# A hybrid mLSTM/RG-LRU block with 32 experts: part of the conditioning scale summed on VectorE, with another order in the first regions

## The chip, the cores and the metric

The kernel runs on one core of one Trainium2 chip. The metric is the time of one execution on the device in microseconds; a kernel's figure is the median of its runs. The profile is that of one execution, and its times count from the first instruction.

## What is computed

One layer of a streaming encoder, on 256 frames of 2048 features, in float32. The part that matters here is the beginning:

```python
mod = jax.nn.silu(c) @ w_ada[l] + b_ada[l]
sh1, sc1, g1, sh2, sc2, g2 = jnp.split(mod, 6, axis=-1)
hn = rmsnorm(x) * (1.0 + sc1[:, None]) + sh1[:, None]
mix = hybrid_mixer(hn, w_in[l], ...)          # proj = hn @ w_in, then mLSTM heads and RG-LRU blocks, then w_out
x = x + g1[:, None] * mix
hn = rmsnorm(x) * (1.0 + sc2[:, None]) + sh2[:, None]
x = x + g2[:, None] * hier_moe(hn, ...)       # 32 experts, the two best of one group for each frame
y = rmsnorm(x) * final_g
```

c is one vector of 2048, w_ada is 2048 x 12288: six conditioning vectors of 2048 features. The scale sc1 (section 1) and the shift sh1 (section 0) are needed before the first product with w_in (2048 x 6152) can be made.

## The kernel before

All weights come through one queue (SyncE) in chunks of 1 MB into a ring of seven buffers; SyncE and TensorE work in the order in which the code is written, VectorE and ScalarE in an order that a scheduler sets when the program is built. It is fixed then: each engine takes its instructions one after the other.

The features of the model dimension are worked in four groups of 512, the regions (kk = 0 to 3). For a group the kernel needs that part of the scale and of the shift, both 512 values. Each is a product of silu(c) with 2048 x 512 of w_ada, 4 chunks. ada_now (L253) makes it on TensorE: per chunk four products in which 32 columns hold one column of cz (silu(c)) and the 512 columns of w_ada pass by, so four partial sums of the row end up on partitions 0, 32, 64 and 96 of one PSUM tile. ada_quarters (L261) then adds the bias row (L264, VectorE) and turns the row into four columns of 128 with four products with one column (L269), which also add the four partial sums; L271 (VectorE) writes them to ada. A product in f32 shows as two instructions in the profile.

x_transposed (L361) transposes the normalised x of the group by TensorE (L366), and ScalarE multiplies by the scale while it copies to xT (L368). modulate (L373) adds the shift: ScalarE writes the rounded sum HH (L375), VectorE what is left, HL (L376). by_channel (L469) is one chunk of w_in: split (L463) makes its rounded half on ScalarE (L465) and its low half on VectorE (L466), each for two of the chunk's four slices at a time, into one of three buffers ws; then 48 products follow, in threes: HH with the rounded half (L481), HL with the rounded half (L482), HH with the low half (L483).

Region 0's scale and shift come first and nothing overlaps them. Then, in region kk = 0, 1 and 2, the kernel makes three chunks of w_in products (go(0), go(1), go(2), for three groups of output columns whose sums stay in PSUM) and in between, by hand-written order, the scale and shift of region kk + 1: eight chunks of w_ada. So a region asks for eleven chunks. The order is go(0), three chunks of the scale, go(1), the fourth, two chunks of the shift, the scale's columns, the transposes, two chunks of the shift, its row, go(2) with the shift's columns and modulate in its middle. In the third of these regions (kk = 2, EARLY) go(2) stands ahead of the last two shift chunks. Region 3 has only its three chunks of w_in. Below, "first", "second" and "third region" are kk = 0, 1 and 2.

Behind that stage come the rest of the products with w_in, the recurrences, the four other sections of the conditioning (ada_later, on VectorE and TensorE, in the buffer acc), w_out, the router, and then the experts in ten rounds, with 32-column products (L1114, L1167) that take their weights straight from the ring.

Of the kernel before, what the change touches and what calls it, by code (L numbers as in the profile page):

```python
# [14 lines left out]
OP = mybir.AluOpType  # L15
# [94 lines left out]
def block_kernel(ctx, tc, x, c, w_ada, b_ada, w_in, b_gates, vec_a, vec_b, w_lru_a, w_lru_x, w_out,  # L110
# [11 lines left out]
    def pb(shape=(128, 512), name="pb"):  # L122
        return psum.tile(list(shape), F32, name=name, tag="b", bufs=2)
# [4 lines left out]
    def st(shape, name, tag=None, bufs=1, dt=F32):  # L128
        return sb.tile(list(shape), dt, name=name, tag=tag or name, bufs=bufs)
# [68 lines left out]
    cs = st([128, NCONST], "cs")  # L198
# [62 lines left out]
    def ada_quarters(sec, n, ps):  # L261
# [8 lines left out]
        one = 1.0 if sec == 1 else 0.0  # L270
        V.tensor_scalar(ada[:, sec, n * 4:n * 4 + 4], pc, one, None, op0=OP.add)  # L271

    def ada_row(sec, k):
        return chunk(w_ada[:, sec * D:sec * D + D].rearrange("(p k) (j n) -> p k j n", k=16, j=4)[:, k])

    acc = st([128, 4, 512], "acc")


    unsummed = []
# [396 lines left out]
    for kk in range(4):  # L676
        go = lambda i, mid=None: by_channel(pss[i], kk, first[i][0], mid)
        if kk == 3:
            for i in range(3):
                go(i)  # L680
            decay()
            SP.dma_start(wlru[:, 0], w_lru_a.rearrange("n c d -> c n d"))
            SP.dma_start(wlru[:, 1], w_lru_x.rearrange("n c d -> c n d"))
            SP.dma_start(cs[:, C_LT:], const[:, C_LT:])
            SP.dma_start(wg, w_in[:, 4096:4104].rearrange("(k p) n -> p k n", p=128))
            SP.dma_start(wr, w_rt.rearrange("(k p) n -> p k n", p=128))
            break
        pss1 = [pb() for _ in range(2)]
        a1, a0 = (ada_now(sec, kk + 1, p) for sec, p in zip((1, 0), pss1))
        q1, q0 = (ada_quarters(sec, kk + 1, p) for sec, p in zip((1, 0), pss1))  # L690
        go(0)
        for _ in range(3):
            next(a1)
        go(1)
        next(a1)
        next(q1)
        next(a1, None)
        next(a0)
        next(a0)
        next(q1, None)  # L700
        x_transposed(4 * kk + 4)
        early = kk in EARLY
        if early:
            go(2)
        next(a0)
        next(a0)
        next(q0)

        def mid():
            next(q0, None)  # L710
            modulate(kk + 1)

        if early:
            mid()
        else:
            go(2, mid)
# [626 lines left out]
```

## Time and profile before

| | us |
|---|---|
| median of 3 runs | 1347.98 (1347.59 to 1357.47) |
| the profiled execution | 1349.25 |
| its span, first to last instruction | 1347.4 |
| TensorE busy | 1161.2 |
| VectorE busy | 545.1 |
| ScalarE busy | 350.5 |

The profiled execution's time is 1.85 us longer than its span. In the profile PE is TensorE, PEld its weight loads, DVE VectorE, ACT ScalarE, SP SyncE. An instruction's row gives its start and its duration; in square brackets stands the time that its engine was idle before it, and what ended that. Matmuls overlap each other, so their pace is read from one start to the next and not from the duration.

### The profile page before, as it was taken

How to read it: one execution, taken by the hardware profiler on the slowest of the kernel's cores; microseconds unless marked ns; L12 is line 12 of the kernel's file. 1: busy time of each engine (PE TensorE's matmuls, PEld its weight loads, DVE VectorE, ACT ScalarE, POOL GpSimd, SP SyncE). 2: the span in 40 equal slices, each digit the busy share in tenths (PEclk: the TensorE clock that was granted, in tenths of full speed). 3: DMA queues.
4: the chain of work that ended last, by engine and by line, in shares of the span. 5: the costliest groups of instructions: out<-in, count | busy, mean ns of one | idle time of the engine just before them, and what ended most of it. 6: DMA issues, size and time to landing. Idle time of an engine off the chain costs nothing. (4 is left out here: it accounts for less than half of the span.)

```text
span 1347.4 us, 19862 instructions
## 1 busy us (share of the span) xinstructions
PE 1161.2 (86%) x8002; PEld 668.1 (50%) x8002; DVE 545.1 (40%) x985; ACT 350.5 (26%) x557; POOL 5.6 (0%) x13
## 2 busy tenths in 40 slices
PE   4898999999999999999777898878885688887886
PEld 0667889987877888543132434223341133422332
DVE  1333667779869877523013131302140013130214
ACT  2232494545446443521010111001010010100103
POOL 0000000000000000000000000000000000000000
PEclk9999999999989999899899999999997889998998
DMA  9999869689969998989999999999997999999995
GB/s 335 375 375 365 270 221 338 239 328 344 365 246 405 408 375 322 359 353 403 423 423 423 422 423 423 423 424 423 424 423 312 424 424 422 423 423 424 423 413 217
DMA packets 116896, 504.81 MB, mean 375 GB/s; under 512 B 12425, under 2 KB 14761, under 8 KB 69185
## 3 DMA queue, kind: packets, MB, share of 16 engines
q1 hardware_dynamic: 114832, 496.97, 92.4%
q0 software_dynamic: 720, 5.24, 0.9%
q8 instruction: 64, 1.05, 0.3%
q10 hardware_dynamic: 1248, 1.29, 0.3%
q14 instruction: 32, 0.25, 0.0%
HBM read 526.54 MB, written 2.10 MB: 392 GB/s over the span
## 5 line engine op out<-in xcount | busy, mean ns | idle before, releaser
L1114 PE MATMUL pa<-ring,XE 128*32 128x512 f32 x1368 | 224.6, 631 | 59.0 <-DMA ring<-in_w_e_up_dram 33.3
L466 DVE TENSOR_TENSOR ws<-ring,ws 128x1024 fp32r<-128x1024 f32 x128 | 154.8, 1219 | 65.1 <-ACT ws L465 64.6
L465 ACT ACTIVATE ws<-ring 128x1024 fp32r<-128x1024 f32 x128 | 134.4, 1058 | 164.8 <-PE pa L497 76.2
L481 PE MATMUL pa<-HH,ws 128*128 128x256 f32 x512 | 151.6, 296 | 3.6 <-ACT ws L465 1.9
L483 PE MATMUL pa<-HH,ws 128*128 128x256 f32 x512 | 148.9, 291 | 5.0 <-DVE ws L466 5.0
L1114 PE MATMUL pa<-early,XE 128*32 128x512 f32 x656 | 135.0, 624 | 20.9 <-DMA early<-in_w_e_up_dram 12.6
L1114 PEld LDWEIGHTS pa<-ring,XE 128*32 128x32 f32 x1368 | 60.1, 115 | 183.4 <-issue 93.2
L482 PE MATMUL pa<-HL,ws 128*128 128x256 f32 x512 | 148.7, 290 | 1.4 <-DVE HL L376 1.4
L1114 PE MATMUL pa<-more,XE 128*32 128x512 f32 x536 | 109.4, 614 | 14.5 <-DMA more<-in_w_e_up_dram 14.5
L977 ACT ACTIVATE XE<-pb,adx 128x128 f32<-128x128 f32 x80 | 36.6, 457 | 304.4 <-DVE XE L980 304.4
L1167 PE MATMUL pa<-ring,hT 128*32 128x512 f32 x640 | 106.0, 598 | 11.1 <-DMA ring<-in_w_e_down_dram 11.0
L1146 DVE TENSOR_TENSOR hs<-hs,pa 128x512 f32<-128x512 f32 x10 | 6.9, 688 | 264.0 <-PE pa L1114 264.0
L481 PEld LDWEIGHTS pa<-HH,ws 128*128 128x128 f32 x512 | 101.8, 199 | 18.5 <-issue 8.4
L483 PEld LDWEIGHTS pa<-HH,ws 128*128 128x128 f32 x512 | 101.7, 199 | 6.6 <-DVE ws L466 6.6
L482 PEld LDWEIGHTS pa<-HL,ws 128*128 128x128 f32 x512 | 101.8, 199 | 2.0 <-DVE HL L376 1.9
L325 DVE SCALAR_TENSOR_TENSOR acc<-ring,cz,acc 128x1024 f32<-128x1024 f32 x78 | 98.1, 1276 | 0.9 <-DMA ring<-in_w_ada_dram 0.8
L1134 DVE TENSOR_TENSOR X<-X,pa 128x512 f32<-128x512 f32 x80 | 51.9, 682 | 91.6 <-PE pa L1132 91.6
L973 PE MATMUL pb<-two,XN 128*128 128x128 f32 x640 | 77.3, 279 | 6.7 <-ACT hT L1153 6.7
L973 PEld LDWEIGHTS pb<-two,XN 128*128 128x128 f32 x640 | 73.1, 192 | 18.9 <-issue 9.2
L1114 PEld LDWEIGHTS pa<-early,XE 128*32 128x32 f32 x656 | 34.0, 113 | 79.5 <-issue 38.1
L1125 ACT ACTIVATE ys<-y 128x512 fp32r<-128x512 f32 x40 | 25.2, 630 | 181.1 <-DVE y L1123 181.1
L1167 PE MATMUL pa<-more,hT 128*32 128x512 f32 x304 | 57.1, 594 | 4.0 <-DMA more<-in_w_e_down_dram 4.0
(378 smaller groups left out, 1379.1 us busy)
## 6 DMA issues: line engine op xcount, KB each, us to landing
ring<-in_w_ada_dram SPq DMA_DIRECT2D x96, 1024.0 KB
ring<-in_w_e_gate_dram SPq DMA_DIRECT2D x62, 1024.0 KB
ring<-in_w_e_down_dram SPq DMA_DIRECT2D x61, 1024.0 KB
ring<-in_w_e_up_dram SPq DMA_DIRECT2D x57, 1024.0 KB
ring<-in_w_in_dram SPq DMA_DIRECT2D x48, 1024.0 KB
early<-in_w_e_up_dram SPq DMA_DIRECT2D x30, 1024.0 KB
more<-in_w_e_down_dram SPq DMA_DIRECT2D x29, 1024.0 KB
more<-in_w_e_up_dram SPq DMA_DIRECT2D x25, 1024.0 KB
```

The lines of the kernel that those rows point to most:

```text
L325: V.scalar_tensor_tensor(o, w[:, h:h + 2], cz[:, k, 3:4], o, op0=OP.mult, op1=OP.add)
L465: A.activation(ws[:, 0], s, AF.Copy)
L466: V.tensor_tensor(ws[:, 1], s, ws[:, 0], op=OP.subtract)
L481: PE.matmul(o, wh[:, cc], HH[:, k], start=k == 0 and ch % 2 == 0, stop=False, skip_group_check=True)
L482: PE.matmul(o, wh[:, cc], HL[:, k], start=False, stop=False, skip_group_check=True)
L483: PE.matmul(o, wl[:, cc], HH[:, k], start=False, stop=k == 15, skip_group_check=True)
L973: PE.matmul(p[:, j], XN[:, h, kk, j], which[:, h], start=h == 0, stop=h == 1)
L977: A.activation(XE[:, k], p[:, j], AF.Identity, scale=adx[:, 1, k:k + 1], bias=adx[:, 0, k:k + 1])
L1114: PE.matmul(o[c0:c0 + width], lhs(kk, j)[:, c0:c0 + width], w[:, j], start=first and j == 0, stop=last and j == 3)
L1125: A.activation(ys[0], y, AF.Copy)
L1134: V.tensor_tensor(X1[:, h, ns], X1[:, h, ns], pc, op=OP.add)
L1167: PE.matmul(pds[n][c0:c0 + width], hT[:, f, c0:c0 + width], w[:, n], start=f == 0, stop=f == 3)
```

## The change

For regions 1 to 3 the scale is no longer a product. ada_vector multiplies each slice of w_ada (128 rows by 512 columns) by its column of cz on VectorE and sums the sixteen slices into acc, which then holds 128 partial sums for each of the 512 features. ada_columns makes columns of them: for each of the four columns one product of the bias row with the column that selects its row, and one of acc with a column of ones, summed in PSUM. The row addition of the scale on VectorE goes. The shift stays as it was.

The order of a region becomes: two chunks of the scale, go(0), two chunks of the scale, one of the shift, go(1), two of the shift, (third region: go(2),) the last of the shift, the scale's columns, the transposes, the shift's row, go(2) with the shift's columns and modulate in its middle.

```diff
+    def ada_vector(sec, n):
+        o = acc[:, n]
+        for kk in range(4):
+            w = ada_w(sec, n, kk)
+            for j in range(4):
+                sc = cz[:, kk * 4 + j, 3:4]
+                if kk + j == 0:
+                    V.tensor_scalar(o, w[:, j], sc, None, op0=OP.mult)
+                else:
+                    V.scalar_tensor_tensor(o, w[:, j], sc, o, op0=OP.mult, op1=OP.add)
+            yield
+
+    def ada_columns(sec, n):
+        pc = pb([128, 4])
+        for j in range(4):
+            js = slice(j * 128, j * 128 + 128)
+            PE.matmul(pc[:, j:j + 1], arow[sec][:, js], cs[:, C_SEL + n:C_SEL + n + 1], start=True, stop=False)
+            PE.matmul(pc[:, j:j + 1], acc[:, n, js], cs[:, C_SEL + 11:C_SEL + 12], start=False, stop=True)
+        one = 1.0 if sec == 1 else 0.0
+        V.tensor_scalar(ada[:, sec, n * 4:n * 4 + 4], pc, one, None, op0=OP.add)
...
-        pss1 = [pb() for _ in range(2)]
-        a1, a0 = (ada_now(sec, kk + 1, p) for sec, p in zip((1, 0), pss1))
-        q1, q0 = (ada_quarters(sec, kk + 1, p) for sec, p in zip((1, 0), pss1))
+        ps0 = pb()
+        a1, a0, q0 = ada_vector(1, kk + 1), ada_now(0, kk + 1, ps0), ada_quarters(0, kk + 1, ps0)
+        for _ in range(2):
+            next(a1)
         go(0)
-        for _ in range(3):
+        for _ in range(2):
             next(a1)
+        next(a0)
         go(1)
-        next(a1)
-        next(q1)
-        next(a1, None)
         next(a0)
         next(a0)
-        next(q1, None)
-        x_transposed(4 * kk + 4)
         early = kk in EARLY
         if early:
             go(2)
         next(a0)
-        next(a0)
+        ada_columns(1, kk + 1)
+        x_transposed(4 * kk + 4)
         next(q0)
```

In the changed kernel the lines lie 21 to 23 further down: the split's halves are L488 and L489 there, the products L504 to L506, HL is L399, the accumulation L283 (first) and L285, the scale's columns L293, L294 and L296.

VectorE at the start of the first region, before; ring_64 is the first chunk of w_in, ws its two halves:

```order
L264 TENSOR_TENSOR row<-pb,brow 128x512
L271 TENSOR_SCALAR ada<-pb 128x4
L466 TENSOR_TENSOR ws<-ring_64,ws 128x1024
L376 SCALAR_TENSOR_TENSOR HL<-xT,ada,HH 128x256 x4
L466 TENSOR_TENSOR ws<-ring_64,ws 128x1024
```

VectorE at the same place in the changed kernel, up to the first w_in chunk, which is ring_66 now; acc is the sum of the scale, ring_64 and ring_65 chunks of w_ada:

```order
L264 TENSOR_TENSOR row<-pb,brow 128x512
L283 TENSOR_SCALAR acc<-ring_64,cz 128x512
L271 TENSOR_SCALAR ada<-pb 128x4
L285 SCALAR_TENSOR_TENSOR acc<-ring_64,cz,acc 128x512
L399 SCALAR_TENSOR_TENSOR HL<-xT,ada,HH 128x256 x4
L285 SCALAR_TENSOR_TENSOR acc<-ring_64,cz,acc 128x512 x2
L285 SCALAR_TENSOR_TENSOR acc<-ring_65,cz,acc 128x512 x4
L489 TENSOR_TENSOR ws<-ring_66,ws 128x1024 x2
```

The low halves of the first w_in chunk stand behind two chunks' accumulations now; one of them stood ahead of HL before.

VectorE from the write of the shift in the middle of the first region's go(2) through the first two w_in chunks of the second region, before:

```order
L271 TENSOR_SCALAR ada<-pb 128x4
L466 TENSOR_TENSOR ws<-ring_68,ws 128x1024
L376 SCALAR_TENSOR_TENSOR HL<-xT,ada,HH 128x256 x4
L466 TENSOR_TENSOR ws<-ring_65,ws 128x1024 x2
L264 TENSOR_TENSOR row<-pb,brow 128x512
L271 TENSOR_SCALAR ada<-pb 128x4
L264 TENSOR_TENSOR row<-pb,brow 128x512
L466 TENSOR_TENSOR ws<-ring_64,ws 128x1024 x2
```

The low half of ring_68 ahead of HL is that of the second region's go(0), ring_65 is its go(1). The same place in the changed kernel, where ring_63 is go(0) and ring_67 go(1):

```order
L271 TENSOR_SCALAR ada<-pb 128x4
L285 SCALAR_TENSOR_TENSOR acc<-ring_68,cz,acc 128x512
L399 SCALAR_TENSOR_TENSOR HL<-xT,ada,HH 128x256 x4
L285 SCALAR_TENSOR_TENSOR acc<-ring_69,cz,acc 128x512 x3
L489 TENSOR_TENSOR ws<-ring_63,ws 128x1024
L285 SCALAR_TENSOR_TENSOR acc<-ring_69,cz,acc 128x512
L489 TENSOR_TENSOR ws<-ring_63,ws 128x1024
L285 SCALAR_TENSOR_TENSOR acc<-ring_64,cz,acc 128x512 x4
L285 SCALAR_TENSOR_TENSOR acc<-ring_65,cz,acc 128x512 x4
L489 TENSOR_TENSOR ws<-ring_67,ws 128x1024 x2
```

Four accumulations and HL stand between the shift's write and go(0)'s first low half, and nine accumulations between that and go(1)'s. The third region has the same pattern.

TensorE behind the first region's go(1), before (L366 are the transposes, L481 the first product of go(2)), and the same place in the changed kernel (L389 are the transposes there, L504 the first product of go(2)):

```order
L258 MATMUL pb<-ring_69,cz 32x512 x4
L258 MATMUL pb<-ring_63,cz 32x512 x4
L258 MATMUL pb<-ring_64,cz 32x512 x4
L269 MATMUL pb<-cs,row 128x1 x4
L366 MATMUL pb<-cs,X 128x128 x8
L258 MATMUL pb<-ring_65,cz 32x512 x4
L258 MATMUL pb<-ring_66,cz 32x512 x4
L481 MATMUL pa<-HH,ws 128x256
```

```order
L258 MATMUL pb<-ring_64,cz 32x512 x4
L258 MATMUL pb<-ring_65,cz 32x512 x4
L258 MATMUL pb<-ring_66,cz 32x512 x4
L293 MATMUL pb<-cs,brow 128x1
L294 MATMUL pb<-cs,acc 128x1
...
L389 MATMUL pb<-cs,X 128x128 x8
L504 MATMUL pa<-HH,ws 128x256
```

Three chunks of the shift instead of five chunks of both lie behind go(1), eight products with one column stand for four, and the transposes are followed by go(2) at once.

## Rows read from the trace of the kernel before

**Rows 1.** The page: busy us (share of the span) and instructions of each engine.
```profile
PE 1161.2 (86%) x8002; PEld 668.1 (50%) x8002; DVE 545.1 (40%) x985; ACT 350.5 (26%) x557; POOL 5.6 (0%) x13
```

**Rows 2.** Busy time by stretches of the span; the columns are in the first line.
```profile
core 0: us, PE busy (x) PEld busy (x) DVE busy (x) ACT busy (x) POOL busy (x), PEclk, DMA share, GB/s
44.00:75.00 31.00, 28.02 (x213) 21.18 (x214) 10.71 (x16) 9.65 (x15) 0.00 (x0) 1.00 1.02 374
106.00:146.00 40.00, 33.90 (x255) 26.79 (x253) 13.40 (x19) 11.97 (x19) 1.05 (x2) 0.91 0.88 297
...
164.00:540.00 376.00, 368.94 (x2250) 310.95 (x2248) 296.35 (x385) 196.58 (x292) 4.35 (x7) 0.98 0.86 325
```

**Rows 3.** Timeline at the start of the first region: start us, us, engine, line, operation.
```profile
39.29 1.05 ACT L465 ACTIVATE ws<-ring 128x1024 fp32r<-128x1024 f32 x1
42.97 0.16 DVE L271 TENSOR_SCALAR ada<-pb 128x4 f32<-128x4 f32 x1 [2.02 <-PE pb L269]
43.24 1.71 ACT L375 ACTIVATE HH<-xT,ada 128x256 fp32r<-128x256 f32 x4 [2.89 <-DVE ada L271]
44.20 1.67 DVE L376 SCALAR_TENSOR_TENSOR HL<-xT,ada,HH 128x256 fp32r<-128x256 f32 x4
45.11 0.41 PE L483 MATMUL pa<-HH,ws 128*128 128x256 f32 x1
```

**Rows 4.** Timeline of the first region from go(1) on, TensorE and the shift's write.
```profile
54.83 0.39 PE L481 MATMUL pa<-HH,ws 128*128 128x256 f32 x1
...
60.77 2.78 PE L258 MATMUL pb<-ring,cz 128*32 128x512 f32 x24
63.48 1.05 PE L269 MATMUL pb<-cs,row 128*128 128x1 f32 x8
...
66.38 0.66 PE L366 MATMUL pb<-cs,X 128*128 128x128 f32 x4 [0.93 <-ACT xT L368]
...
70.84 0.39 PE L483 MATMUL pa<-HH,ws 128*128 128x256 f32 x1 [1.43 <-DVE ws L466]
...
73.56 0.95 PE L269 MATMUL pb<-cs,row 128*128 128x1 f32 x8
74.37 0.36 PE L481 MATMUL pa<-HH,ws 128*128 128x256 f32 x1
74.54 0.16 DVE L271 TENSOR_SCALAR ada<-pb 128x4 f32<-128x4 f32 x1 [1.49 <-PE pb L269]
```

**Rows 5.** Timeline of TensorE from the third region's go(2) on.
```profile
131.04 0.58 PE L481 MATMUL pa<-HH,ws 128*128 128x256 f32 x1 [1.87 <-ACT ws L465]
132.30 0.58 PE L483 MATMUL pa<-HH,ws 128*128 128x256 f32 x1 [0.47 <-DVE ws L466]
...
140.06 1.92 PE L258 MATMUL pb<-ring,cz 128*32 128x512 f32 x16
142.80 1.05 PE L269 MATMUL pb<-cs,row 128*128 128x1 f32 x8 [0.81 <-DVE row L264]
```

**Rows 6.** VectorE's groups by shape: count, busy us, mean ns of one, idle before.
```profile
L466 DVE TENSOR_TENSOR ws<-ring,ws 128x1024 fp32r<-128x1024 f32 x109 | 132.1, 1219 | 52.2 <-ACT ws L465 52.0
L325 DVE SCALAR_TENSOR_TENSOR acc<-ring,cz,acc 128x1024 f32<-128x1024 f32 x78 | 98.1, 1276 | 0.9 <-DMA ring<-in_w_ada_dram 0.8
...
L323 DVE TENSOR_SCALAR acc<-ring,cz 128x1024 f32<-128x1024 f32 x8 | 5.9, 748 | 3.3 <-PE pa L285 3.3
...
L652 DVE SCALAR_TENSOR_TENSOR TO<-TO,XG 128x512 f32<-128x512 f32 x4 | 2.6, 682 | 0.0
```

**Rows 7.** TensorE's timeline ahead of the regions, where products wait for chunks.
```profile
29.45 1.93 PE L258 MATMUL pb<-ring,cz 128*32 128x512 f32 x8 [0.68 <-DMA ring<-in_w_ada_dram]
32.16 1.94 PE L258 MATMUL pb<-ring,cz 128*32 128x512 f32 x8 [0.78 <-DMA ring<-in_w_ada_dram]
```

**Rows 8.** Busy time by stretches in which the granted clock fell; columns as in rows 2.
```profile
130.20:137.00 6.80, 5.50 (x24) 5.21 (x25) 3.50 (x3) 2.67 (x3) 0.00 (x0) 0.50 1.08 331
...
147.20:150.70 3.50, 3.50 (x19) 3.50 (x18) 0.05 (x1) 0.12 (x1) 0.00 (x0) 0.51 1.01 320
232.60:239.40 6.80, 6.80 (x33) 6.80 (x33) 4.98 (x9) 2.70 (x5) 0.00 (x0) 0.50 0.93 373
```

More of the change, by code (lines that the diff above doesn't have):

```diff
@@ L271, in ada_quarters @@
         V.tensor_scalar(ada[:, sec, n * 4:n * 4 + 4], pc, one, None, op0=OP.add)
+    acc = st([128, 4, 512], "acc")
+    def ada_vector(sec, n):
[17 more added lines that the diff above has]
+        V.tensor_scalar(ada[:, sec, n * 4:n * 4 + 4], pc, one, None, op0=OP.add)
     def ada_row(sec, k):
         return chunk(w_ada[:, sec * D:sec * D + D].rearrange("(p k) (j n) -> p k j n", k=16, j=4)[:, k])
-    acc = st([128, 4, 512], "acc")
     unsummed = []
```

## Prediction

> **What bounds the kernel now.** I read the page first: TensorE is busy 86% of the span [rows 1], so the question is where its work sets the end. The view by stretches [rows 2] answers it. From 164 to 540 us TensorE is busy 368.94 of 376 us, so whatever time it gains or loses before 164 us arrives at the experts, whose start it sets, and behind them at the end. In the changed part (regions of about 31 us: 44 to 75, 75 to 106, and 106 to 146 with the tail) TensorE is busy 28.02 of 31.00 us and 33.90 of 40.00 us, while the DMA engines show a share of 1.02 and 0.88. So in a region two things are close to full: TensorE, and the transfers. VectorE is busy 10.71 of 31 us there. That looks like room, but an engine that works in order can hold TensorE up with 35% load if the wrong thing stands ahead in its queue; so I next read the timeline of the first region [rows 3, 4] for what each first product waits for, and the order of VectorE in both kernels.
>
> A region is three chunks of w_in, each 48 products, and eight chunks of w_ada. 48 products start at 54.83 and end at 60.77: 0.124 us each. Three w_ada chunks run from 60.77 to 63.48: 0.90 us each. The four products with one column take 0.95 to 1.05 us [rows 4].
>
> **The change, part by part.**
>
> 1. Products removed and added. In each of three regions four chunks of the scale leave TensorE: 12 x 0.90 = -10.8 us. The four products with one column become eight, so 3 x 0.95 = +2.9 us. Net -7.9 us, all of it on the path if nothing else waits.
>
> 2. VectorE's new work. Per region 16 operations on 128x512: one tensor_scalar and 15 scalar_tensor_tensor. The same form over 128x1024 takes 1276 ns, and one over 128x512 elsewhere 682 ns [rows 6]; bounds 0.64 (half of the first) and 0.69, and I take 0.68. The first, by 748 ns for twice its size, takes 0.4. Sum 10.6 us per region, and the row addition of the scale (0.69) goes. VectorE then works about 21 of 31 us, so it isn't full; what counts is what stands behind these operations.
>
> 3. Start of the first region. Today ada is written at 42.97, HH and HL follow, and the first product that needs the low half of the split weights (L483) runs at 45.11 [rows 3]. That chunk was there before 39.29, when ScalarE splits it without a wait for it. In the new order two w_ada chunks are fetched ahead of it: 2 x 2.7 us (two neighbouring products that wait for chunks start at 29.45 and 32.16 [rows 7]), so it is there by 44.7; ScalarE splits it after the four HH, at 46.0, and that isn't late. VectorE is: behind ada (43.13) stand one accumulation, four HL (1.67), six accumulations and the low half (1.22): 43.13 + 0.68 + 1.67 + 6 x 0.68 + 1.22 = 50.8. TensorE gets its third product at 50.8 instead of 45.11: +5.7 us (5.4 to 5.9 with the bounds of 2). The third chunk's eight accumulations cost nothing more here: VectorE is through with them and the next low half 7.9 us later (1.22 + 8 x 0.68 + 1.22), TensorE needs it after 8.2 (7.0 for the rest of this first chunk as in the trace, 0.90, 0.25).
>
> 4. First chunk of the second and third region. Let T be the end of ada's write by L271 in the middle of the third chunk of the region before (74.70 in the trace). TensorE has 24 products left from 74.37, so it needs the next low half at T + 2.9. VectorE has one accumulation, four HL, three accumulations and the low half ahead: 0.68 + 1.67 + 2.04 + 1.22 = 5.6. A wait of 2.7 us.
>
> 5. Second chunk of these regions. From that low half VectorE has an accumulation, the other low half, eight accumulations and the next low half: 0.68 + 1.22 + 5.44 + 1.22 = 8.6 us. TensorE has 46 products, one w_ada chunk and two products: 5.7 + 0.90 + 0.25 = 6.8. A wait of 1.7 us. Items 4 and 5 together: 2 x 4.4 = +8.8 us. Bounds: nothing, if VectorE's operations were done while it is idle now, and 9.4 us with 0.69 us each and 0.1 us between engines. I take 8.8, since queue and durations are known.
>
> 6. The transposes. They move behind the last w_ada chunk. Today two w_ada chunks lie between them and the third w_in chunk and cover ScalarE's copies and split; the wait is 1.43 us at 70.84. In the third region that cover is missing already and the waits are 1.87 and 0.47 us [rows 4, 5]. The new order makes the first two regions like that: 2 x 0.9 = +1.8. In the third region the w_in chunk now runs ahead of the transposes, so its 2.3 us go; the 0.81 us for the row of the shift at 142.80 goes too, since transposes lie above it. Together -1.3 us (bounds -3 and +2: what waits follow the eight products with one column isn't in the trace).
>
> 7. The queues. SyncE issues the same 44 chunks in another order; half of the w_ada chunks are now set free by VectorE instead of TensorE. A chunk for VectorE stays in its buffer until its four accumulations are done, up to 5.4 us behind the low half. By the pace of 2.7 us the chunks of w_in arrive some microseconds ahead of their use as counted above, so I cost this at nothing; if that cover is gone, a late buffer shows as ScalarE's split waiting for w_in, up to 2.7 us a region. Behind the last region, what VectorE and ScalarE do is the same apart from a few neighbours that swap places.
>
> Sum: 5.7 - 7.9 + 8.8 - 1.3 = +5.3 us. The profiled execution took 1349.25 us (span 1347.4 and 1.85 around it), 1.27 above the median of 1347.98; on the execution that is 1354.6, on the median 1353.3. I say 1353.
>
> **A rule weighed against the trace.** The granted clock is 0.50 (1.2 GHz) from 130.2 to 137.0, right behind waits of 1.87 and 0.47 us, and 0.51 from 147.2 to 150.7, behind more waits; it is also 0.50 from 232.6 to 239.4, where TensorE is busy 6.80 of 6.80 us [rows 8]. The Trainium skill (TensorE: Matmul & The Clock Gate, "What's actually happening") says that the default state is throttled and activity releases it. The first two rows agree with that, the third doesn't; by the rule each new wait would lower the clock and the sum would be that of rival C, by the rows the falls come either way and the sum stands.
>
> **The rivals.**
>
> A (forecast). VectorE's queue gives back more than the products saved: 1353, between 1348 and 1359. For it: the order of VectorE is fixed and the durations are measured. Chance 0.63.
>
> B. The queue does no harm in the second and third region: items 4 and 5 fall away, 5.3 - 8.8 = -3.5 us, 1344.5. For it: VectorE idles two thirds of a region today; it would have to reach the accumulations earlier than its order allows, or TensorE be late for another reason. Against it: three accumulations and four HL stand between ada and the low half. Chance 0.20.
>
> C. The clock. TensorE gets six new or longer waits of 1.7 us and more (two each by items 4, 5 and 6). After the wait at 131.04, 46 products took 132.30 to 140.06 = 7.8 us instead of 5.7 [rows 5, 4]: 2.1 us per fall. With four falls more the sum is 5.3 + 8.4 = 13.7, and with all six 17.9: 1362 to 1366. It decides, as slower by over 1%, from four on. Against it: after the waits of 0.93 and 1.43 us at 66.38 and 70.84 products still came at the fast pace, and a part of a slow stretch is hidden in the next wait for VectorE. Chance 0.08.
>
> D. The transfers set the pace and the change does not do what it says. Eleven chunks of 2.7 us are 29.8 us of a region's 31.0, whoever uses them, so at most 1.2 us a region is to be had and the new waits lie beside the transfers: 3 x -1.2 = -3.6 at best, and nothing at worst: 1344 to 1348. For it: a DMA share of 1.02. Against it: with items 3 to 5 TensorE is the later one. Chance 0.09.
>
> **How the numbers follow.** A measurement of this kernel tells about 1% (13.5 us) from no change. A, B and D lie inside of it: 0.92, less 0.01 for the end of A's tail and 0.02 for the product saving of 7.9 us and noise with it on the fast side: within 1% 0.89, slower by over 1% C with A's tail, 0.09, faster 0.02. The range takes in A with its tail, and of B and D the greater part: 1345 to 1360; C and the fast part of B are left out. A's own range is 1348 to 1359.
>
> **What would show it.** Right: the first L483 product of the first region (now L506) near 50.8; in the next two regions waits of TensorE for VectorE's low half of about 2.7 and 1.7 us, twice each; the last product of this stage some 5 us later than today; the stage to 540 as full as before. Wrong: no such waits in the second region (B); ScalarE's split waiting for w_in in each region (D); a granted clock of 0.5 in more stretches between 50 and 150 us than the two of today (C). The forecast fails if TensorE enters the stage behind 164 us earlier than now, or if its loss there is not found again at the end.

## The result, and the profile after

| | before | after |
|---|---|---|
| median | 1353.30 (1347.42 to 1357.52, 19 runs) | 1357.57 (1353.72 to 1366.64, 19 runs) |
| ratio | | 1.0052, 95% interval 1.0034 to 1.0071 |
| the profiled execution | 1349.25 (span 1347.4) | 1356.01 (span 1354.2) |

The changed kernel is 0.5% slower by the ratio of all the runs; the two medians alone stand at 1.0032. The executions of the kernel before lie in two groups, 1347.4 to 1350.8 and 1353.2 to 1357.5, which is why its median of three was 1347.98 and its median of 19 is 1353.30. Ratios below are against the kernel before as run on the same chip in the same turn.

The page of the changed kernel, busy us of each engine, against [rows 1]:

```profile
PE 1160.2 (86%) x7930; PEld 667.1 (49%) x7930; DVE 577.3 (43%) x1030; ACT 350.9 (26%) x557; POOL 5.6 (0%) x13
```

VectorE has 32 us more, and TensorE 72 instructions but only 1.0 us less. Twelve chunks of products should have taken 10.8 us away. The changed part says why; the same two stretches as in [rows 2]:

```profile
core 0: us, PE busy (x) PEld busy (x) DVE busy (x) ACT busy (x) POOL busy (x), PEclk, DMA share, GB/s
44.00:75.00 31.00, 22.58 (x160) 18.62 (x161) 19.07 (x26) 7.76 (x11) 0.00 (x0) 0.78 1.05 386
164.00:540.00 376.00, 370.37 (x2296) 313.28 (x2295) 300.56 (x395) 201.18 (x298) 4.36 (x7) 0.99 0.86 327
```

From 44 to 75 us TensorE gets 160 instructions done instead of 213, at a mean granted clock of 0.78 instead of 1.00 (what the 1.00 leaves out is said below). Behind 164 us it is as full as before.

The start of the first region, the counterpart of [rows 3]:

```profile
42.31 0.16 DVE L271 TENSOR_SCALAR ada<-pb 128x4 f32<-128x4 f32 x1 [0.81 <-PE pb L269]
42.39 0.74 DVE L285 SCALAR_TENSOR_TENSOR acc<-ring,cz,acc 128x512 f32<-128x512 f32 x1
...
43.12 1.68 DVE L399 SCALAR_TENSOR_TENSOR HL<-xT,ada,HH 128x256 fp32r<-128x256 f32 x4
...
44.72 4.68 DVE L285 SCALAR_TENSOR_TENSOR acc<-ring,cz,acc 128x512 f32<-128x512 f32 x6
...
45.28 0.58 PE L504 MATMUL pa<-HH,ws 128*128 128x256 f32 x1 [3.01 <-ACT ws L488]
...
49.32 2.35 DVE L489 TENSOR_TENSOR ws<-ring,ws 128x1024 fp32r<-128x1024 f32 x2
...
50.59 0.58 PE L506 MATMUL pa<-HH,ws 128*128 128x256 f32 x1 [4.51 <-DVE ws L489]
```

VectorE goes without a pause from ada through one accumulation, HL and six more accumulations to the low half; TensorE gets its third product at 50.59 instead of 45.11. The same thing from the first region's go(2) into the second region, VectorE alone:

```profile
79.29 0.16 DVE L271 TENSOR_SCALAR ada<-pb 128x4 f32<-128x4 f32 x1 [2.49 <-PE pb L269]
79.37 0.74 DVE L285 SCALAR_TENSOR_TENSOR acc<-ring,cz,acc 128x512 f32<-128x512 f32 x1
80.09 1.69 DVE L399 SCALAR_TENSOR_TENSOR HL<-xT,ada,HH 128x256 fp32r<-128x256 f32 x4
81.70 2.32 DVE L285 SCALAR_TENSOR_TENSOR acc<-ring,cz,acc 128x512 f32<-128x512 f32 x3
83.93 1.22 DVE L489 TENSOR_TENSOR ws<-ring,ws 128x1024 fp32r<-128x1024 f32 x1
85.07 0.74 DVE L285 SCALAR_TENSOR_TENSOR acc<-ring,cz,acc 128x512 f32<-128x512 f32 x1
85.73 1.22 DVE L489 TENSOR_TENSOR ws<-ring,ws 128x1024 fp32r<-128x1024 f32 x1
86.87 6.26 DVE L285 SCALAR_TENSOR_TENSOR acc<-ring,cz,acc 128x512 f32<-128x512 f32 x8
93.04 2.36 DVE L489 TENSOR_TENSOR ws<-ring,ws 128x1024 fp32r<-128x1024 f32 x2
```

And what TensorE makes of it, its pauses from the first region's transposes to the third region's second w_in chunk:

```profile
72.49 0.58 PE L504 MATMUL pa<-HH,ws 128*128 128x256 f32 x1 [2.17 <-ACT ws L488]
...
73.75 0.58 PE L506 MATMUL pa<-HH,ws 128*128 128x256 f32 x1 [0.47 <-DVE ws L489]
...
85.20 0.58 PE L506 MATMUL pa<-HH,ws 128*128 128x256 f32 x1 [2.44 <-DVE ws L489]
...
94.31 0.39 PE L506 MATMUL pa<-HH,ws 128*128 128x256 f32 x1 [0.61 <-DVE ws L489]
...
107.78 0.39 PE L504 MATMUL pa<-HH,ws 128*128 128x256 f32 x1 [2.17 <-ACT ws L488]
...
109.04 0.58 PE L506 MATMUL pa<-HH,ws 128*128 128x256 f32 x1 [0.76 <-DVE ws L489]
...
120.00 0.39 PE L506 MATMUL pa<-HH,ws 128*128 128x256 f32 x1 [2.44 <-DVE ws L489]
...
129.10 0.58 PE L506 MATMUL pa<-HH,ws 128*128 128x256 f32 x1 [1.92 <-DVE ws L489]
```

The 2.44, 0.61, 2.44 and 1.92 us are the two waits of items 4 and 5, in both regions. The 2.17 us stand between the transposes and go(2).

The other half of the story is the granted clock (columns as above; compare [rows 8]):

```profile
43.80:54.00 10.20, 4.21 (x18) 3.92 (x19) 9.92 (x15) 2.44 (x5) 0.00 (x0) 0.50 1.05 387
71.10:77.90 6.80, 4.94 (x21) 4.65 (x22) 4.26 (x5) 2.29 (x4) 0.00 (x0) 0.50 1.05 387
84.70:88.10 3.40, 2.90 (x13) 2.90 (x14) 3.37 (x5) 0.00 (x0) 0.00 (x0) 0.51 0.28 66
108.60:112.00 3.40, 2.96 (x14) 2.96 (x15) 3.33 (x5) 0.07 (x1) 0.00 (x0) 0.51 1.06 386
129.10:132.50 3.40, 3.40 (x16) 3.40 (x17) 2.22 (x2) 0.94 (x1) 0.00 (x0) 0.50 1.03 342
149.60:156.40 6.80, 5.93 (x25) 5.62 (x26) 2.54 (x8) 2.40 (x6) 0.00 (x0) 0.50 0.91 214
```

From 40 to 160 us the clock is recorded at 1.2 GHz, half of its upper level, for 34 us, against 10.2 us before (6.8 and 3.4, [rows 8]). Five of these six stretches begin in or right behind a pause of 1.9 us or more, the sixth (149.6) behind the third region's transposes and pauses of 0.26 and 1.08 us. Not every such pause is followed by a fall: behind the 2.44 us that end at 120.00 the clock stays at 1.00 up to 129.1.

The rows leave out a slow start of the kernel before. They say 1.00 for it from the beginning, but its products come at half pace, 0.21 us from one start to the next, up to 48.3 us, and at 0.12 us from there:

```profile
47.88 0.41 PE L481 MATMUL pa<-HH,ws 128*128 128x256 f32 x1
...
48.43 0.28 PE L481 MATMUL pa<-HH,ws 128*128 128x256 f32 x1
```

In the changed kernel TensorE was at full pace by 41.3 us (eight one-column instructions take 1.02 us there, and 1.84 us at 41.1 in the kernel before) and fell back at 43.8. So from the third product to the next stage the kernel before has about 13 us at half pace, and the changed one 27.

The stage ends, and the next begins, at the first product of the recurrence, first in the kernel before, then in the changed one:

```profile
168.19 1.89 PE L544 MATMUL pb<-XG,wlru 128*128 128x256 f32 x8
```

```profile
174.55 1.67 PE L567 MATMUL pb<-XG,wlru 128*128 128x256 f32 x7
```

That is 6.4 us later; the span is 6.8 us longer. "Next stage" below means this product. That the two numbers are so close is partly luck: at the router's first product, ahead of the experts, the changed kernel is only 3.7 us behind (557.89 against 554.16, shown with e6 below). Between 160 and 560 us its clock is low for 14 us, that of the kernel before for 20, which is worth 3.4 us at half pace; behind it another 3 us are lost again.

### The profile page after: what moved, and what is told of

The parts are those of the page before. It is cut to its first block, busy times and chain, and to the rows that moved or that the text cites. A ratio compares the mean times of both kernels' runs of the same rounds, so it can differ in the third digit from the quotient of the medians.

```text
span 1354.2 us, 19763 instructions
## 1 busy us (share of the span) xinstructions
PE 1160.2 (86%) x7930; PEld 667.1 (49%) x7930; DVE 577.3 (43%) x1030; ACT 350.9 (26%) x557; POOL 5.6 (0%) x13
## 2 busy tenths in 40 slices
DMA packets 116897, 504.83 MB, mean 373 GB/s; under 512 B 12424, under 2 KB 14760, under 8 KB 69184
## 5 line engine op out<-in xcount | busy, mean ns | idle before, releaser
L1135 PE MATMUL pa<-ring,XE 128*32 128x512 f32 x1368 | 227.5, 637 | 55.5 <-DMA ring<-in_w_e_up_dram 31.7
L489 DVE TENSOR_TENSOR ws<-ring,ws 128x1024 fp32r<-128x1024 f32 x128 | 155.0, 1221 | 69.0 <-ACT ws L488 67.0
L488 ACT ACTIVATE ws<-ring 128x1024 fp32r<-128x1024 f32 x128 | 134.7, 1060 | 178.1 <-PE pa L520 76.9
L506 PE MATMUL pa<-HH,ws 128*128 128x256 f32 x512 | 150.3, 294 | 14.7 <-DVE ws L489 14.7
L504 PE MATMUL pa<-HH,ws 128*128 128x256 f32 x512 | 152.5, 298 | 8.6 <-ACT ws L488 7.7
L1135 PE MATMUL pa<-early,XE 128*32 128x512 f32 x656 | 138.3, 633 | 22.2 <-DMA early<-in_w_e_up_dram 13.8
L504 PEld LDWEIGHTS pa<-HH,ws 128*128 128x128 f32 x512 | 102.5, 200 | 23.2 <-ACT ws L488 13.0
L506 PEld LDWEIGHTS pa<-HH,ws 128*128 128x128 f32 x512 | 102.4, 200 | 16.9 <-DVE ws L489 16.9
L1188 PE MATMUL pa<-more,hT 128*32 128x512 f32 x304 | 60.7, 622 | 5.3 <-DMA more<-in_w_e_down_dram 5.3
```

Source lines behind the costliest of these rows:

```text
L488: A.activation(ws[:, 0], s, AF.Copy)
L489: V.tensor_tensor(ws[:, 1], s, ws[:, 0], op=OP.subtract)
L504: PE.matmul(o, wh[:, cc], HH[:, k], start=k == 0 and ch % 2 == 0, stop=False, skip_group_check=True)
L506: PE.matmul(o, wl[:, cc], HH[:, k], start=False, stop=k == 15, skip_group_check=True)
L1135: PE.matmul(o[c0:c0 + width], lhs(kk, j)[:, c0:c0 + width], w[:, j], start=first and j == 0, stop=last and j == 3)
L1188: PE.matmul(pds[n][c0:c0 + width], hT[:, f, c0:c0 + width], w[:, n], start=f == 0, stop=f == 3)
```

## The experiments

Each changes the beginning alone. "Next stage" and "slow" are read from one profiled execution of each kernel, the ratio from all its runs. "Slow" is the time recorded at a granted clock of 0.5 between 40 and 165 us, worked out from stretches of 1.7 us; "half pace to" is where a slow start of the products as above ends that these rows leave out, and a dash means that TensorE was at full pace by 42 us.

| run | next stage, us | slow, us | half pace to, us | ratio to before |
|---|---|---|---|---|
| before | 168.19 | 10 | 48.3 | 1 |
| after | 174.55 | 34 | - | 1.0052 (1.0034 to 1.0071) |
| e1: sums, order of before | 184.87 | 42 | 47.9 | 1.0110 (1.0077 to 1.0143) |
| e2: products, new order | 173.22 | 24 | 45.8 | 0.9998 (0.9977 to 1.0019) |
| e3: first region as before | 169.09 | 20 | 48.2 | 0.9998 (0.9976 to 1.0020) |
| e4: low halves first | 166.08 | 24 | 53.5 | 0.9996 (0.9974 to 1.0019) |
| e6: low halves first, transposes covered | 160.43 | 14 | 47.4 | 1.0010 (0.9981 to 1.0040) |
| e7: the same, third go(2) early | 163.19 | 17 | 49.1 | 1.0019 (0.9996 to 1.0043) |
| e8: after, transposes covered | 175.79 | 37 | - | 1.0060 (1.0032 to 1.0087) |
| e9: after, pauses filled | 176.98 | 20 | 46.1 | 1.0043 (1.0021 to 1.0066) |
| e10: e6, pauses filled | 161.98 | 14 | - | 0.9975 (0.9953 to 0.9997) |

**e1 and e2: the two halves of the change, alone.** e1 sums on VectorE in the order of before:

```diff
-        for _ in range(2):
+        go(0)
+        for _ in range(3):
             next(a1)
-        go(0)
-        for _ in range(2):
-            next(a1)
-        next(a0)
         go(1)
+        next(a1)
         next(a0)
         next(a0)
+        ada_columns(1, kk + 1)
+        x_transposed(4 * kk + 4)
...
-        ada_columns(1, kk + 1)
-        x_transposed(4 * kk + 4)
+        next(a0)
         next(q0)
```

> The scale summed on VectorE, but the chunks, the transposes and the columns in the order of the kernel before. In VectorE's queue the low half of the second w_in chunk of each region stands behind twelve accumulations (8.2 us). Theory (VectorE's queue gives back more than the products saved): in each region a wait of about 6 us for that low half, the first recurrence product of the next stage about 10 us later than in the kernel before (168.2 there), time 0.6 to 1.0% above before. Rival 1 (the new order of the chunks and transposes is to blame, the sums are a gain): 4 to 8 us earlier than before, ratio 0.994 to 0.998. Rival 2 (the transfers set the pace): within 3 us of before.

e2 makes the scale by products, in the new order:

```diff
-        ps0 = pb()
-        a1, a0, q0 = ada_vector(1, kk + 1), ada_now(0, kk + 1, ps0), ada_quarters(0, kk + 1, ps0)
+        pss1 = [pb() for _ in range(2)]
+        a1, a0 = (ada_now(sec, kk + 1, p) for sec, p in zip((1, 0), pss1))
+        q1, q0 = (ada_quarters(sec, kk + 1, p) for sec, p in zip((1, 0), pss1))
...
+        next(q1)
         next(a0)
         go(1)
...
-        ada_columns(1, kk + 1)
+        next(q1, None)
```

> The new order of chunks and transposes, but the scale by products on TensorE as before. Theory: the order alone costs 2 us at the start of the first region (the chunk of w_in comes two chunks later) and 0.9 us each in two regions, and saves 3 us in the third: the next stage begins within 2 us of 168.2, ratio 0.998 to 1.002. Rival 1 (the order is to blame): 5 us or more later than before, ratio 1.004 and more.

In e1 the three chunks between go(0) and go(1) put twelve accumulations ahead of go(1)'s low half. The pauses in front of it, from TensorE's timeline:

```profile
56.10 0.58 PE L506 MATMUL pa<-HH,ws 128*128 128x256 f32 x1 [4.58 <-DVE ws L489]
...
93.89 0.58 PE L506 MATMUL pa<-HH,ws 128*128 128x256 f32 x1 [4.43 <-DVE ws L489]
...
131.68 0.58 PE L506 MATMUL pa<-HH,ws 128*128 128x256 f32 x1 [4.43 <-DVE ws L489]
```

They are shorter than the 6 us expected, but the next stage comes 16.7 us later than before, where 10 were expected, and the kernel is 1.1% slower: the new order is what makes the sums bearable. e2 has no sums and still reaches the next stage 5.0 us late, more than expected: its pauses between transposes and go(2) are 2.17 and 0.53, 2.17 and 0.46, 2.62 and 0.62 us, with three falls of the clock of 6.8 us there. Its third product comes 2.4 us later than before (47.46). From there to the next stage its pauses add up to 11.5 us, as in the kernel before (11.6), but the w_in products take 84.5 us instead of 79.7. So in this execution the order has its own price, by the start and by the clock behind the transposes. The time does not show these 5 us: the interval of the ratio ends at 1.0019 (2.6 us), and the profiled execution is the slowest of e2's twelve (1356.71).

**e3: the start.** The first region's code is that of before, the other two as changed.

```diff
+        if kk == 0:
+            pss1 = [pb() for _ in range(2)]
+            a1, a0 = (ada_now(sec, kk + 1, p) for sec, p in zip((1, 0), pss1))
...
+        else:
+            ps0 = pb()
+            a1, a0, q0 = ada_vector(1, kk + 1), ada_now(0, kk + 1, ps0), ada_quarters(0, kk + 1, ps0)
...
```

> The first region is made as in the kernel before (scale by products, its order); the second and third region are as changed. Theory (the start of the first region costs 5.5 us by VectorE's queue, less the 0.9 us products that it saves there): first product with a low half back near 45.1 us, second region's first product near 77 to 78 us instead of 82.1, next stage's first product near 169 to 171 us instead of 174.55, time 0.2 to 0.3% above before. Rival (the start's loss is covered by something else, such as transfers): the second region starts as late as in the changed kernel, next stage near 174, time 0.5% above before.

The third product is at 44.74, the next stage at 169.09, 5.5 us earlier than in the changed kernel, and the time can't be told from that of before. So the first region is nearly all of the loss, and its start alone is 5.5 us (50.59 against 45.11); the other two regions together come out about even, what they save in products going into their waits and clock. e3 puts back the whole first region, its order as well as its scale, and doesn't part the two.

**e4 and e5: VectorE's queue.** e4 keeps the order of SyncE and TensorE but writes VectorE's by hand: the low halves of w_in go ahead of the accumulations that aren't due yet. e5 keeps the queue and halves what stands in it.

```diff
         for j in range(4):
+            if j % 2 == 0:
+                ws = split(w[:, j:j + 2])
             if mid and j == 2:
                 mid()
-            if j % 2 == 0:
-                ws = split(w[:, j:j + 2])
...
+        if kk == 0:
+            fetch(1, 0)
+            fetch(1, 1)
+            accum(2)
+        go(0, lambda: accum(2))
+        accum(4 if kk == 0 else 2)
+        fetch(kk + 1, 2)
+        fetch(kk + 1, 3)
```

> The changed kernel's chunks, transposes and products in the same order on SyncE and TensorE, with VectorE's order written by hand: the low halves of each w_in chunk ahead of the accumulations, four accumulations of the next region in the middle of the third chunk. Same work. Theory (queue): the third product of the first region at 48 instead of 50.6 us, the waits of 2.44 us fall to under 1, those of 0.61 and 1.92 go; the next stage begins at 165 to 167 instead of 174.6, time 0.1 to 0.3% below before. Rival 1 (order of chunks and transposes) and rival 3 (VectorE's load, wherever it stands): within 2 us of the changed kernel, ratio 1.004 to 1.006. Rival C (clock): the waits go and the clock still falls five times before 160 us, half of the gain is missing.

```diff
+    V.memset(acc, 0.0)
...
-                    V.scalar_tensor_tensor(o, w[:, j], sc, o, op0=OP.mult, op1=OP.add)
+                    V.scalar_tensor_tensor(o[:, :256], w[:, j, :256], sc, o[:, :256], op0=OP.mult, op1=OP.add)
```

> The changed kernel with each accumulation over 256 of its 512 columns, the other columns left out of the scale's sum; order and everything else the same. An operation takes about 0.48 instead of 0.68 us. Theory (queue): third product of the first region 1.4 us earlier, the waits of 2.44 us about 1.6, those of 0.61 and 1.92 gone; next stage 5 us earlier than in the changed kernel, near 169, ratio to before 1.000 to 1.003. Rival 1 (order of chunks and transposes): as the changed kernel, ratio 1.004 to 1.006.

e5 leaves out the products of half of the scale's features. The router then picks other experts (the transfers grow from 504.83 to 529.98 MB), so its total (1415.99 us) tells nothing. Its beginning does: the next stage is at 169.73, near the 169 expected; go(1) has no wait; go(0) of the second and third region waits 1.64 us, as expected; the third product is at 47.86, 2.7 us earlier, where 1.4 were expected (0.8 of them lie ahead of ada). An accumulation over 256 columns takes 484 ns. In e4:

```profile
48.03 0.58 PE L523 MATMUL pa<-HH,ws 128*128 128x256 f32 x1 [1.09 <-DVE ws L506]
...
166.08 0.38 PE L584 MATMUL pb<-XG,wlru 128*128 128x256 f32 x1
```

The order in VectorE's queue alone is worth 8.5 us at the next stage (174.55 to 166.08) and turns 0.5% slower into no change; the 0.1 to 0.3% below before that were expected don't show. This shows the mechanism: the same work, the same transfers, another order on an engine that is 43% busy. It isn't the clock: the third product comes 2.6 us earlier and the pauses behind it are 9.0 us instead of 15.1, while the w_in products take 84.5 us, about as long as in the changed kernel (85.1).

**e6 and e7: cover for the transposes too.** e6 splits the next region's first w_in chunk ahead of modulate, fetches one scale chunk in go(2)'s middle, and puts two shift chunks between transposes and go(2) in all regions; e7 makes the third region's go(2) ahead of the transposes.

```diff
         ada_columns(1, kk + 1)
         x_transposed(4 * kk + 4)
+        if not early:
+            next(a0)
+        next(a0)
         next(q0)
...
+            ahead.append(begun(kk + 1, first[0][0]))
             next(q0, None)
             modulate(kk + 1)
...
```

> Sums on VectorE, with w_in's low halves ahead of the accumulations by hand, and the transposes covered by two chunks of the shift. Theory (the waits, and the falls of the granted clock behind them, are what the change gives back): no wait over 1 us in front of go(1) or go(2), at most two stretches of clock 0.5 between 45 and 165 us, next stage's first product at 160 to 164 us, time 0.3 to 0.6% below before. Rival (the transfers set the pace once TensorE's waits are gone): waits for chunks take their place, next stage near 166 to 168, time as before.

> As the run with low halves first and the transposes covered, but the third region's go(2) is made ahead of the scale's columns and the transposes, so those and the shift's row have no cover behind them. Theory: some 2 us more of waits behind that go(2) and one more fall of the clock there, next stage's first product 2 to 4 us later than with all covered. Rival (the third region's tail is hidden by the split and the transfers): no difference over 1 us.

e6 reaches the next stage at 160.43 as expected, 7.8 us ahead of before, e7 at 163.19, 2.8 later than e6, as expected too. But neither is faster. Not as expected, e6 still waits 1.5 us for the low half in two go(2) and 3.12 us in front of the third, with three falls of the clock instead of two at most.

Where did e6's lead go? The router's first product, in before, in the changed kernel and in e6:

```profile
554.16 0.38 PE L973 MATMUL pb<-two,XN 128*128 128x128 f32 x1
```

```profile
557.89 0.38 PE L994 MATMUL pb<-two,XN 128*128 128x128 f32 x1
```

```profile
550.13 0.38 PE L1030 MATMUL pb<-two,XN 128*128 128x128 f32 x1
```

4.0 us are left there, and e6's span is 1347.7 us, 0.3 longer than before's. From 160 us to that product e6's clock is low for 23.9 us, 20.5 in before: 3.4 us more at half pace, which explain 1.7 of the 3.7 us lost. In the experts its last 4 us go. The transfers are full there in both kernels (DMA share 1.01 from 700 to 900 us), and behind 560 us the clock is low for 94 us in e6 and for 76 in before; which of the two takes the lead isn't settled. The prediction's premise, that whatever TensorE gains or loses ahead of 164 us arrives at the end, holds about for the losses of e1 and of the changed kernel (16.7 and 6.4 us at the next stage, 18.0 and 6.8 at the end), but not for the leads of e6 and e7.

**e8 and e9: is it the pause that lowers the clock?** e8 is the changed kernel with columns and transposes moved directly behind go(1), so two shift chunks cover them. e9 puts products nobody reads into the pauses.

```diff
         go(1)
+        ada_columns(1, kk + 1)
+        x_transposed(4 * kk + 4)
         next(a0)
         next(a0)
...
-        ada_columns(1, kk + 1)
-        x_transposed(4 * kk + 4)
```

> The changed kernel with one thing moved: the scale's columns and the transposes stand directly behind go(1), so the two next chunks of the shift lie between them and go(2), as in the kernel before; VectorE's work is the same. Theory (the pause of 2.2 and 0.5 us between transposes and go(2) costs itself and a fall of the clock behind it): that pause goes in the first two regions (some 1.8 us each) and the clock's falls at 71 and 109 us with it (some 2 and 1.5 us), while the waits for the low half of 2.44 us at the start of the second and third region and the 5.5 us of the start stay; next stage's first product at 167 to 169 us instead of 174.55, time 0.1 to 0.2% above before. Rival (the clock falls without the pause as well): only the pauses go, next stage near 171, time 0.3% above before.

```diff
+    def filler(ps, m):
+        for _ in range(m):
+            PE.matmul(ps, ident, X[:, 0, 0:512], start=True, stop=True)
...
+        filler(ps0, (8, 2, 2)[kk])
         go(0)
...
         next(q0)
+        filler(ps0, (2, 2, 1)[kk])
```

> The changed kernel with products put into TensorE's pauses whose result nobody reads (128x512, about 0.8 us each): eight ahead of the first region's go(0), two ahead of go(0) of the second and third region, two between the transposes and go(2) of the first two regions, one behind the transposes of the third. They are shorter than the pauses that they stand in, so they make nothing later by themselves. Theory (the clock falls because TensorE pauses): the stretches of clock 0.5 that begin at 43.8, 71, 84, 108 us go, at most two are left between 40 and 165 us, the 598 split products of the stage take 79 to 81 us instead of 85.1, next stage's first product near 169 to 171 us instead of 174.55, time about 0.2% above before. Rival (the falls come whether TensorE pauses or not): as many falls, next stage at 174 us or later.

e8 agrees with neither expectation: the 2.17 us are gone, yet the next stage is at 175.79. The falls are still there, and the waits for the low half at the start of the second and third region have grown from 2.44 to 3.23 us: what TensorE gains ahead of a wait for VectorE it waits longer. Two stretches of e8 in which the transposes and shift products stand, without a pause over 1 us:

```profile
67.70:71.10 3.40, 3.40 (x20) 1.23 (x24) 0.00 (x0) 2.71 (x4) 0.00 (x0) 0.64 0.72 259
...
103.00:106.40 3.40, 3.40 (x20) 1.25 (x24) 0.00 (x0) 2.38 (x4) 0.00 (x0) 0.53 0.03 13
```

e9 splits the question. Three of its stretches:

```profile
43.80:54.00 10.20, 10.20 (x40) 6.08 (x39) 9.92 (x15) 2.86 (x5) 0.00 (x0) 1.00 1.05 387
...
69.00:75.80 6.80, 5.62 (x17) 3.08 (x17) 2.85 (x4) 3.57 (x6) 0.00 (x0) 0.57 1.05 386
84.70:88.10 3.40, 1.60 (x13) 1.39 (x13) 3.37 (x5) 0.15 (x1) 0.00 (x0) 1.00 0.58 168
```

The 1.00 from 43.8 on is a start that the rows leave out: the first instructions of the fill come at half pace (0.85 us apart), and from 46.3 on they come 0.43 us apart, while TensorE works without a pause:

```profile
42.11 3.76 PE L290 MATMUL pb<-X,cs 128*128 128x512 f32 x4
...
46.30 4.88 PE L290 MATMUL pb<-X,cs 128*128 128x512 f32 x11
```

So with the pause filled TensorE is at full pace by 46.3 us. The changed kernel, whose code differs in the fill alone, is there at 54.0, and e4 at 53.5; both pause at this place. At 84.7 the fill shortens the pause from 2.44 to 1.80 us, and no fall follows. Behind 69 the clock falls all the same, by 70.2, behind the sixteen one-column instructions and the first transposes and ahead of the fill; three falls are left, where two at most were expected. So falls come with pauses, and also with columns and transposes and the short pauses between them. The w_in products of the stage take 78.6 us in e9 instead of 85.1, as expected; the next stage isn't earlier because the fill was too long: behind the first region's start 18 of its instructions took 832 ns in the mean, the first eight products held go(0) to 50.62, and those at 72.27 ran at half pace. That part of the expectation, that they make nothing later, was wrong.

**e10: e6 with its pauses filled.**

```diff
         next(q0)
+        filler(ps0, (2, 2, 4)[kk])
```

> The run with low halves first and the transposes covered, with two such products (third region: four) ahead of go(2). Theory: its falls at 94 and 128 us go, next stage's first product at 157 to 159 us instead of 160.4. The lead over the kernel before is then 9 to 11 us at that point; whether it is still there at the start of the experts (554 us) and at the end tells whether the stages behind give it back: by the run without these products about a quarter of it reaches the experts and nothing the end, so time as before; if the loss there was only that run's clock, time 0.3 to 0.6% below before.

The next stage is at 161.98, later than e6 and later than expected (the fill waits 0.82 us for the shift's row); the falls near 95 and 126 stay. But the router starts earlier than in e6:

```profile
546.70 0.38 PE L1035 MATMUL pb<-two,XN 128*128 128x128 f32 x1
```

7.5 us ahead of before, and the span is 1341.8 us, 5.6 shorter. It is the only version faster than both kernels, 0.25% by the ratio (medians 1346.38 and 1349.84), by an interval that ends at 0.9997. Its clock is low for 10 us between 160 and 560, where e6 had 27. Whether the fill does this, or this execution was lucky with the clock, these runs don't tell: the profiled execution is the fastest of e10's twelve (1343.60), and the intervals of e6 and e10 overlap.

## Why the prediction was right or wrong

The forecast was 5 us slower than before, by VectorE's queue; measured were 0.5% (7 us on before's median; 4.3 us between the medians; 6.8 us in the two profiled executions). Sign, places and the queue held, and 1357.57 lies in the range. Two steps failed: the clock, which the sum put at nothing (below), and the reading of the sum as no change. About 1% was called what a measurement tells, and 19 runs of each tell 0.2%, so that a slowdown of the forecast size is a clear one. And 1353 was counted from a median of three runs that lay 5.3 us below that of 19.

Step by step, from the third product to the next stage: 45.11 to 168.19 is 123.1 us before, 50.59 to 174.55 is 124.0 us after. The parts are worked out from the starts of the instructions in these stretches, pauses set apart.

1. Products: the chunks of w_ada go from 22.1 to 11.3 us, the forecast 10.8; the one-column products from 5.8 to 9.0, +3.2 where 2.9 was forecast.
2. VectorE's operations were mis-sized: 0.75 us each, outside of the bounds of 0.64 to 0.69 (the changed kernel first, then the kernel before).

```profile
L285 DVE SCALAR_TENSOR_TENSOR acc<-ring,cz,acc 128x512 f32<-128x512 f32 x45 | 33.8, 750 | 1.2
```

```profile
L1306 DVE SCALAR_TENSOR_TENSOR X<-X,r,pb 128x512 f32<-128x512 f32 x4 | 2.7, 744 | 0.0
```

The rows of the prediction were half of a wider instruction, and one whose factor is a constant (L652). The kernel before has this operation with a column as factor: L1306 over 512 columns takes 744 ns, HL (L376) over 256 takes 480, and the accumulation over 1024 takes 1276. The three lie on a line, by estimate 0.21 us and 1.04 ns a column, so half of the widest leaves out half of the fixed part. The 45 accumulations make 3 us more of VectorE's time than forecast.

3. The start was right: 50.59 for 50.8, +5.5 for +5.7. Two errors cancel: seven operations of 0.07 us more, and ada 0.7 us earlier than the kernel before had it.
4. The waits at the second and third region's first chunk: 2.44 us twice for 2.7. From the end of ada's write (79.45) to the third product 5.75 us pass, 5.6 were forecast; TensorE was through with its products after 3.3 (82.76) instead of 2.9, so the wait is 0.3 us shorter.
5. At their second chunk: 0.61 and 1.92 us for 1.7. VectorE needs 9.1 us between the two low halves in both regions (85.20 to 94.31, 120.00 to 129.10), forecast 8.6. The 0.61 is not a gain: in the second region 13 of go(0)'s 48 products ran at 1.2 GHz (84.7 to 88.1) and used up 1.3 us of the wait; in the third region, where go(0) stayed at the upper level, it is 1.92. Items 4 and 5 together were 7.4 us for 8.8.
6. Transposes: before's pauses (0.26, 0.93 and 1.43 us in each of the first two regions, 4.34 in the third) become 2.64, 2.93 and 1.34, together -2.7 us for -1.3, inside the bounds. The item missed that eight transposes in a row no longer wait 0.93 us between their halves. It says nothing of the clock behind the pause.
7. Transfers: TensorE waits for no chunk. Right.

The step that failed is "by the rows the falls come either way and the sum stands". The w_in products of the stage, 598 instructions in both kernels, take 85.1 us instead of 79.7 with the pauses left out: +5.4 us by the clock, a term that the sum had at zero. As measured the sum is 5.5 - 7.6 + 7.4 - 2.7 + 5.4 - 1.6 = 6.4 us, where 5.3 was forecast. The last term is what the sum didn't have either: 0.4 us less for the transposes, and 1.2 us less of the waits that the kernel before has at 144.65, 146.12 and 165.45. So the total came out near by luck: the pauses grew by 3.5 us (11.6 to 15.1) where 7.5 (8.8 - 1.3) were forecast, and these 4 us nearly pay for the clock. About 1.3 of them are the clock's own doing, since what it takes ahead of a wait for VectorE shortens that wait. Rival C was right that the falls come with the waits, four more recorded between 40 and 160 us (six stretches for two), and wrong that each then costs 2.1 us in full; the first of the six stands where the kernel before has its slow start.

The rule weighed there, that the default state of the clock is throttled and activity releases it (the Trainium skill, TensorE: Matmul & The Clock Gate, "What's actually happening"), agrees with e9, where full pace came 8 us earlier with the pause filled. The third row, 232.6 to 239.4 in the kernel before, at 0.50 with TensorE busy throughout, was taken as standing against it; but the fall begins in a run of 32 one-column instructions:

```profile
229.95 4.38 PE L578 MATMUL pb<-cs,sq 128*128 128x1 f32 x32
```

The same run stands in all twelve kernels here, and in eight the clock falls in it or within 1.4 us of its end. So the row is weak evidence that falls come whatever the change does: the change doubles the one-column products ahead of the transposes.

Rival B is refuted by the four waits. Rival D is refuted by e6, which reaches the next stage 7.8 us ahead of before with the same chunks, so the transfers were not the pace. That the change does what it says is shown by item 1.

## What to carry to other kernels

Work given to an idle engine costs what it delays in that engine's queue: list what stands ahead of the instruction that the full engine waits for, at each hand-over. Here 8.5 us at the next stage lay in the order of VectorE's queue alone. Price TensorE's clock as a term of its own: look at what the engine did ahead of each recorded fall, pauses and one-column instructions both, and take off what the next wait swallows. Take an operation's time from a row of its own form, with the same kind of factor, and not from half of a wider one.

## What the runs showed of the hardware that was not expected

The granted clock mostly answered to pauses of TensorE of 1.9 us and more: in the changed kernel it was 0.50 for 3.4 to 10.2 us at five of the six places with such a pause, and not at 120.00; in e9, with the first of them filled with useless products, TensorE was at full pace by 46.3 us instead of 54.0. It also fell behind sixteen one-column instructions and eight transposes without a longer pause (by 70.2 in e9, in the stretches from 67.7 and 103.0 in e8): of the 29 places in these kernels with sixteen such instructions ahead of the transposes, 27 have a fall within 4 us, many of them with a pause of about 2 us as well. It did not fall there behind the eight one-column instructions of the kernel before in its first two regions. No run here parts the columns, the transposes and the short pauses between them.

The clock rows say 1.00 ahead of the first recorded change, also where products come at half pace (up to 48.3 us in the kernel before): the start needs the pace of the products as a second reading.
